# The gate projection of 2048 columns as one Strassen block with 1024-wide halves, in place of two plain jobs and one block with 512-wide halves

## The chip, the cores and the metric

The kernel runs on one core of one Trainium2 chip. The metric is device time in microseconds (us), the median of several executions. The engines are PE (matrix products), DVE (vector work), ACT (scalar work and casts), POOL and SP; in this kernel the last two mostly issue DMAs. Each engine takes its instructions strictly in the order in which they stand in its own program.

## The reference

One decoder layer for 512 rows of 2048 fp32 values. Only the last lines belong to the change:

```
x2  = x + merged @ w_out
g   = sigmoid(x2 @ w_ple_gate)          # 512 x 2048 times 2048 x 2048
x3  = x2 + g * (p @ w_ple)
out = x3 / sqrt(mean(x3^2) + 1e-6) * final_g
```

## The kernel before

**Arithmetic.** Every fp32 product is made of three products on PE: both operands are split into a rounded high part and a rest, and high·high, high·low and low·high are added in PSUM. A weight's high part is a cast on ACT (`hi`, `hs`, `th`, line 191), its low part a subtraction on DVE (`lo`, `ls`, `tl`, line 197). One matmul has 128 rows of x2 (a "row tile" t, four in all) by 512 columns.

**Jobs.** A projection is cut into jobs, which one generator, `gemm`, turns into a single stream of matmuls. A plain job ("N") has 512 columns and runs over 16 slices k of 128 rows of the weights: 16 x 4 x 3 = 192 matmuls. A Strassen job ("S") takes two halves of columns, two halves of the depth and two halves of the rows, and makes 7 products of sums of blocks in place of 8 products of blocks. Its work comes in units of 12 matmuls (one product, two slices k, two row tiles), and each unit needs one weight tile of 128x1024 (512 KB), which is a block of w_ple_gate or a sum of blocks. The gate projection is three jobs: `pg0` (plain, columns 0 to 511), `pg1` (Strassen, columns 512 to 1535 as two halves of 512, 28 units, 336 matmuls) and `pg3` (plain, the last 512): 720 matmuls.

**Order.** `fill(n)` lets the generator run n steps of three matmuls, and the lines between two calls stand in the program at that place. `split_to(i)` issues the cast and the subtraction for a unit two units ahead of its matmuls; there are three buffers for `hs`, three for `ls` and three for raw weights, so a cast waits until PE is through with the unit three before it. `background` is a queue of small pieces that `pop` takes out during the matmuls, `deferred` holds pieces for the next unit. The sums of x2 that Strassen's products need on the activation side are made by DVE in the background, and partly go through DRAM. SP issues the weight loads as raw buffers come free. During the mixers, `slow_one` issues one DMA at a time on POOL that forms sums of weights in DRAM for the output projection and others (line 411 paces it).

**End.** `pg3` is built with `tail=8`: the last 8 slices k are split in advance (`th`, `tl`), and the matmuls then go row tile by row tile, 24 for each t. After each of them `evac_last` runs: tanh on ACT, two operations on DVE that add the gated embedding onto x2 (`ple_add`, lines 1039 and 1042), the sum of squares (ACT, line 1082), a square root (line 1090), a reciprocal (DVE, line 1091), four multiplications by the root and `final_g` (line 1097), and the output's DMAs. Tanh and square root need different function tables on ACT, so there are table loads (lines 1080 and 1113, each issued by a `warm` operation on one column). Row tiles 0 to 2 are finished while PE works on the next. For the last row tile the products with `final_g` are made ahead (`final_weigh`, line 1066). After the last gate matmul PE only has `probe`, 41 small matmuls that nothing waits for.

## Time and profile before

| | |
|---|---|
| median of three executions | 1507.71 us (1507.51 to 1508.45) |
| span of the profiled execution | 1505.6 us |
| PE busy | 1499.0 us (100%) |
| DVE busy | 1244.3 us (83%) |
| ACT busy | 869.2 us (58%) |
| POOL busy | 390.4 us (26%) |

The span runs from the first to the last instruction of the profiled execution; the median is 2.1 us above it. Matmuls are pipelined, so a busy PE is not PE at its peak. A row of the trace gives the start, the duration, the engine, the source line, the operation, and output and input by the program's names; in brackets stands the idle time of the engine just before it and what ended it.

### The profile page before, as it was taken

The page shows a single profiled execution, that of the slowest core. Times are in us where ns is not written, and L with a number is a line of the kernel's source. Part 1 is how long each engine was busy: PE and PEld are TensorE (multiplying, and loading weights), DVE is VectorE, ACT ScalarE, POOL GpSimd, SP SyncE. Part 2 cuts the span into 40 slices and gives each one's busy share as a digit, 9 for nine tenths or more (in the row PEclk, how much of TensorE's full clock was granted, in tenths as well). Part 3 has the DMA queues.
Part 4 walks back from the last instruction along what each step waited for, and adds up shares of the span by engine and source line. Part 5 has one row for each costly group of instructions (what it writes and reads, how often), then busy time and mean ns, then how long its engine had stood idle before and what let it go on. Part 6 is the DMA issues. An engine that isn't in the chain of part 4 may idle for free.

```text
span 1505.6 us, 20508 instructions
## 1 busy us (share of the span) xinstructions
PE 1499.0 (100%) x7190; PEld 1253.5 (83%) x7190; DVE 1244.3 (83%) x1882; ACT 869.2 (58%) x1501; POOL 390.4 (26%) x608
## 2 busy tenths in 40 slices
PE   9999999999999999999999999999999999999998
PEld 8988888888888888888888888888888888888886
DVE  7987879999997888878888888887877985688877
ACT  6554567777765555555665555555546555444556
POOL 1321044343432332432343424330100011100000
PEclk9999999999999999999999999999999999999999
DMA  8889579789877795978595959896897779945555
GB/s 320 218 240 297 149 171 219 167 192 272 189 196 251 222 289 152 280 176 253 149 293 157 281 156 286 247 290 235 295 322 248 229 195 348 307 164 183 182 201 190
DMA packets 183703, 346.82 MB, mean 230 GB/s; under 512 B 15016, under 2 KB 75056, under 8 KB 180400
## 3 DMA queue, kind: packets, MB, share of 16 engines
q0 software_dynamic: 70544, 172.61, 41.9%
q1 hardware_dynamic: 112912, 172.64, 35.7%
q8 instruction: 56, 0.92, 0.2%
q14 instruction: 47, 0.39, 0.1%
q10 hardware_dynamic: 144, 0.26, 0.0%
HBM read 283.08 MB, written 109.58 MB: 261 GB/s over the span
## 4 chain that ended last, share of the span: by engine, by line
PE 98%; DVE 1%; ACT 1%; issue 0%; POOL 0%; POOLq 0%; ACTq 0%
PE ps_m L455 7%; PE ps_m L454 7%; PE ps_m L453 7%; PE ps_wo L454 3%; PE ps_wo L453 3%; PE ps_wo L455 3%; PE ps_t L1477 2%; PE ps_za L480 2%; PE ps_za L481 2%; PE ps_za L482 2%; PE ps_q L480 2%; PE ps_q L481 2%; PE ps_q L482 2%; PE ps_kv L453 2%; PE ps_kv L454 2%; PE ps_kv L455 2%
## 5 line engine op out<-in xcount | busy, mean ns | idle before, releaser
L197 DVE TENSOR_TENSOR ls<-b,hs 128x1024 fp32r<-128x1024 f32 x224 | 273.6, 1222 | 111.0 <-ACT hs L191 109.8
L191 ACT CAST hs<-b 128x1024 fp32r<-128x1024 f32 x224 | 235.5, 1053 | 204.2 <-PE ps_m L455 50.7
L191 ACT CAST hs<-raw 128x1024 fp32r<-128x1024 f32 x130 | 137.0, 1055 | 132.5 <-issue 33.7
L197 DVE TENSOR_TENSOR ls<-raw,hs 128x1024 fp32r<-128x1024 f32 x130 | 158.7, 1221 | 45.8 <-ACT hs L191 45.5
L453 PE MATMUL ps_m<-hs,act_h 128*128 128x512 f32 x256 | 100.1, 391 | 0.0
L455 PE MATMUL ps_m<-hs,act_l 128*128 128x512 f32 x256 | 99.7, 389 | 0.0
L454 PE MATMUL ps_m<-ls,act_h 128*128 128x512 f32 x256 | 99.6, 389 | 0.0
L333 DVE TENSOR_TENSOR b<-raw,b 128x1024 f32<-128x1024 f32 x76 | 92.5, 1218 | 1.6 <-DMA raw<-in_w_in_dram 1.6
L197 DVE TENSOR_TENSOR lo<-raw,hi 128x512 fp32r<-128x512 f32 (+1 forms) x120 | 79.7, 668 | 15.1 <-PE ps_pg L494 5.5
L191 ACT CAST hi<-raw 128x512 fp32r<-128x512 f32 (+1 forms) x120 | 70.6, 596 | 30.1 <-PE ps_pg L495 10.7
L333 DVE TENSOR_TENSOR b<-b,b 128x1024 f32<-128x1024 f32 x72 | 87.6, 1217 | 0.0
L191 ACT CAST pth<-ps_t 128x512 fp32r<-128x512 f32 (+1 forms) x88 | 47.6, 544 | 46.4 <-PE ps_t L1477 45.8
L1436 ACT ACTIVATE prob<-prob,st 128x512 f32<-128x512 f32 (+3 forms) x128 | 70.7, 556 | 5.2 <-DVE st L1427 5.1
L197 DVE TENSOR_TENSOR ptl<-ps_t,pth 128x512 fp32r<-128x512 f32 (+1 forms) x88 | 55.5, 635 | 7.9 <-ACT pth L191 7.2
L411 POOL COPY pad_r<-pad_r 128x1 f32<-128x1 f32 x39 | 31.0, 794 | 115.9 <-ACT pad_r L410 115.9
L1427 DVE CUSTOM_DVE_ANT_0 prob<-ps_s,b 128x512 f32<-128x512 f32 (+3 forms) x128 | 56.1, 484 | 4.4 <-PE ps_s L1418 4.1
L455 PEld LDWEIGHTS ps_m<-hs,act_l 128*128 128x128 f32 x256 | 48.0, 188 | 10.0
L454 PEld LDWEIGHTS ps_m<-ls,act_h 128*128 128x128 f32 x256 | 48.1, 188 | 9.9
L453 PEld LDWEIGHTS ps_m<-hs,act_h 128*128 128x128 f32 x256 | 48.1, 188 | 9.9
L480 PE MATMUL ps_za<-act_h,hi 128*128 128x512 f32 x128 | 54.0, 421 | 0.0
L1452 DVE TENSOR_SCALAR prob<-prob,st,gates 128x512 f32<-128x512 f32 (+3 forms) x128 | 51.8, 457 | 1.8
L480 PE MATMUL ps_q<-act_h,hi 128*128 128x512 f32 x128 | 52.1, 407 | 0.0
(752 smaller groups left out, 4554.4 us busy)
## 6 DMA issues: line engine op xcount, KB each, us to landing
raw<-in_w_in_dram SPq DMA_DIRECT2D x112, 512.0 KB, 5.5
b<-in_w_in_dram SPq DMA_DIRECT2D x58, 512.0 KB, 6.9
o<-in_w_out_dram POOLq DMA_DIRECT2D x48, 512.0 KB, 7.7
t<-in_w_up_b_dram POOLq DMA_DIRECT2D x24, 512.0 KB, 9.9
raw<-in_w_ple_gate_dram SPq DMA_DIRECT2D x24, 512.0 KB, 3.9
b<-o SPq DMA_DIRECT2D x18, 512.0 KB, 6.2
o<-o POOLq DMA_DIRECT2D x16, 512.0 KB, 6.3
act_l<-gate POOLq DMA_DIRECT2D x8, 1024.0 KB, 12.7
```

Source lines behind the costliest of these rows:

```text
L191: nc.scalar.copy(hi, src)
L197: nc.vector.tensor_tensor(out=lo, in0=src, in1=hi.bitcast(F32), op=ALU.subtract)
L333: nc.vector.tensor_tensor(out=b[o], in0=b[x], in1=b[y], op=ALU.subtract)
L453: nc.tensor.matmul(o, ah, wh, start=st, stop=False, skip_group_check=go)
L454: nc.tensor.matmul(o, ah, wl, start=False, stop=False, skip_group_check=go)
L455: nc.tensor.matmul(o, al, wh, start=False, stop=sp, skip_group_check=go)
L480: nc.tensor.matmul(ps, hi[:, j], ah, start=st, stop=False)
L481: nc.tensor.matmul(ps, hi[:, j], al, start=False, stop=False)
L482: nc.tensor.matmul(ps, lo[:, j], ah, start=False, stop=sp)
L1427: nc.vector.tensor_tensor_reduce(out=pt[:, j * n:j * n + n], in0=o[:, j], in1=b0[:, 512 - n:], scale=-SLOPE[h], scalar=3.0e38, op0=ALU.add ...
L1436: nc.scalar.activation(sl, sl, AF.Exp, bias=st[:, 0, j, hh:hh + 1], scale=-1.0, accum_out=st[:, 1, j, hh:hh + 1])
L1452: nc.vector.tensor_scalar(out=sl, in0=sl, scalar1=st[:, 1, j, hh:hh + 1], scalar2=gates[:, i, gate:gate + 1], op0=ALU.mult, op1=ALU.mult)
```

## The change

The three jobs become one Strassen job `pg` whose halves are 1024 columns wide. Each product now has 8 weight tiles u = 0 to 7 (four pairs of slices k, two blocks cb of 512 columns). The list `WIDE` gives the order of 52 units, and product 4's second column block comes at the end as four weight tiles split in advance, row tile by row tile, for rows 256 to 511 only. That is 52 x 12 + 2 x 24 = 672 matmuls.

Where the weight tiles come from: products 1, 2 and 3 use plain blocks. Product 7 reads `gate_sums`, which 16 more POOL DMAs (`slow_one`) form in DRAM during the mixers; each mixer group has two more places for them. b11+b12 for product 5 is added by DVE for u below 4 and by a DMA that adds into SBUF for the other four (tag "T"). Product 6 adds b22 by DVE (line 356), product 4 adds b21 by an adding DMA on POOL (line 441). The sums of x2 are now made from tiles `whole`, copied out of PSUM by ACT.

The output is finished in quadrants: a (rows 0 to 255, columns 0 to 1023), b (same rows, other columns), c (rows 256 to 511, columns 1024 on) and d (the rest). Quadrants a, b and c get their tanh, embedding and squares in the background, and rows 0 to 255 are multiplied and stored in the background too (`roots`, `put_row`). Rows 256 to 511 are finished at the end by `end_row`, once for each of two row tiles.

```diff
+WIDE = ([(p, u) for us in (range(4), range(4, 8)) for p in "21" for u in us] + [("5", u) for u in range(8)]
+        + [(p, u) for u in range(8) for p in "63"] + [("7", u) for u in range(8)] + [("4", u) for u in (0, 2, 4, 6)])
...
+            if job.wide is not None and k == "1" and n < 4:
+                load_to(ld["b12", n])
+                t = raw[ld["b12", n]]
+                nc.vector.tensor_tensor(out=t, in0=t, in1=raw[ld["b11", n]], op=ALU.add)
+            if job.wide is not None and k == "6":
+                nc.gpsimd.dma_start(raw[ld["b12", n]], wide_weights(job, "b21", n), accum_op=ALU.add)
...
+    def wide_units(job, si):
...
+        for n, (p, u) in enumerate(order):
+            flush()
+            split_to(si + state["ahead"] + max(0, n - len(order) + 4))
+            run_behind()
+            pop()
...
+        split_to(si + 3)
+        tails = [parts.pop(si + j) for j in range(4)]
+        for t in range(2):
+            o = sets[0][2 + t]
+            for k in range(8):
...
+                flush()
+                pop()
+                yield
+            job.tail(o, t)
...
+    def finish_last(t, cb, ps):
...
+        nc.scalar.activation(sg, ps, AF.Tanh, scale=0.5)
+
+        def add_on():
+            ple_add(x2, ple, sg)
+            nc.scalar.activation(sg, x2, AF.Square, accum_out=ss[:, 2 + t, 2 * cb:2 * cb + 1])
+        if cb:
+            add_on()
+        else:
+            deferred.append(add_on)
...
+    def put_row(t, half):
+        o = wide_rows("xab"[0] + "ab"[half])[:, t]
+        nc.vector.scalar_tensor_tensor(out=o, in0=o, scalar=rest[:, 0, t:t + 1], in1=columns_g(half), op0=ALU.mult, op1=ALU.mult)
+        nc.sync.dma_start(out[t * P:t * P + P, 1024 * half:1024 * half + 1024], o)
...
+    def end_row(ps, t):
...
+        finish_last(t, 1, ps)
         nc.scalar.activation(warm, eps_t, AF.Sqrt)
...
-    add_job(Job("pg0", "N", w_ple_gate, 0, 512, KT, h_act, evac_first, zs))
-    add_job(Job("pg1", "S", w_ple_gate, 512, 512, KT, gate_act, evac_quad(final_sg, place_sg), ("o", "s", "t")))
-    add_job(Job("pg3", "N", w_ple_gate, 1536, 512, KT, h_act, evac_last, ("s", "s", "g", "g"), tail=8))
+    pg = Job("pg", "S", w_ple_gate, 0, 512, KT, gate_act, evac_wide, (("o", "s"), ("t", "g")), order=WIDE, bank_of=WIDE_BANK, wide=gate_sums)
+    pg.tail = end_row
+    add_job(pg)
...
+    slow.extend(lambda u=u: nc.gpsimd.dma_start(gate_sums[:, u], wide_weights(jobs[-1], "b22", u)) for u in range(8))
+    slow.extend(lambda u=u: nc.gpsimd.dma_start(gate_sums[:, u], wide_weights(jobs[-1], "b12", u), accum_op=ALU.add) for u in range(8))
...
+        if n == 43:
+            assert not background
+            background.extend([nothing, partial(roots, 0)] + [partial(put_row, t, half) for t in range(2) for half in range(2)])
...
+    background.extend([nothing] * 8 + [partial(weigh_rows, "c", 1), partial(weigh_rows, "d", 1, slice(0, 512))])
+    finish("pg")
```

ACT before, the end of its program for the third row tile and the start of the last (`sg` is the tanh's output, `p_h_13627` the x2 tile of the last 512 columns):

```order
L1079 ACTIVATE sg<-ps_pg_13480 128x512
L1080 ACT_TABLE_LOAD
L1080 ACTIVATE warm<-eps_t 128x1
L1082 ACTIVATE sg,small<-p_h_13627 128x512
L1090 ACTIVATE rs<-small,rs 128x1
L1113 ACT_TABLE_LOAD
L1113 ACTIVATE warm<-eps_t 128x1
L1079 ACTIVATE sg<-ps_pg_13481 128x512
```

The table load and its `warm` stand between a row tile's tanh and its square here.

ACT after, the end of its program from the last cast of the tail on (`ps_pg_12715` and `ps_pg_12716` are product 4's first column block for the two row tiles, `ps_pg_12746` its second block for t=0):

```order
L196 CAST ob_h<-b_12938 128x1024
L1197 ACTIVATE sg<-ps_pg_12715 128x512
L1197 ACTIVATE sg<-ps_pg_12716 128x512
L1166 ACTIVATE p_h_13569,small<-p_l_13449 128x1024
L1201 ACTIVATE sg,small<-x 128x512 x2
L1166 ACTIVATE p_h_13569,small<-p_l_13449 128x1024
L1197 ACTIVATE sg<-ps_pg_12746 128x512
L1201 ACTIVATE sg,small<-x 128x512
L1236 ACT_TABLE_LOAD
L1236 ACTIVATE warm<-eps_t 128x1
L1241 ACTIVATE small<-small 128x1
```

Four squares (line 1166 twice, line 1201 twice) now stand between the last cast and the tanh of the row tile t=0, and the table load stands behind that row tile's square, where before it stood ahead of it.

DVE before, from the last weight splits to the first row tile's reciprocal:

```order
L197 TENSOR_TENSOR tl<-raw,th 128x512 x5
L1066 TENSOR_TENSOR p_l_13223<-p_l_13223,p_h_13542 128x512
L1066 TENSOR_TENSOR x_1_13474<-x_1_13474,p_h_13542 128x512
L1074 TENSOR_REDUCE rs<-small 128x4
L1075 TENSOR_SCALAR rs<-rs 128x4
L1039 SCALAR_TENSOR_TENSOR sg<-sg,s_13540 128x512
L1042 SCALAR_TENSOR_TENSOR p_h_13627<-sg,p_h_13627 128x512
L1066 TENSOR_TENSOR p_l_13301<-p_l_13301,p_h_13542 128x512
L1091 RECIPROCAL rs<-rs 128x1
```

The last five subtractions of weights stand together, and the products with `final_g` for the last row tile (line 1066) stand ahead of the first row tile's reciprocal.

DVE after, the same stretch (line 202 with `s_13452` or `p_h_13453` is a tail part's subtraction, line 1221 a `put_row`, lines 1154 and 1155 are `ple_add`):

```order
L202 TENSOR_TENSOR ls<-b_12929,hs 128x1024
L1221 SCALAR_TENSOR_TENSOR p_h_13004<-p_h_13004,small,p_h_13180 128x1024
L202 TENSOR_TENSOR ls<-b_12935,hs 128x1024
L202 TENSOR_TENSOR s_13452<-b_12581,ob_h 128x1024
L1154 SCALAR_TENSOR_TENSOR p_h_13569<-p_h_13569,s_13255 128x1024
L1155 SCALAR_TENSOR_TENSOR p_l_13449<-p_h_13569,p_l_13449 128x1024
L202 TENSOR_TENSOR s_13452<-b_12654,ob_h 128x1024
L202 TENSOR_TENSOR p_h_13453<-b_12932,ob_h 128x1024
L1154 SCALAR_TENSOR_TENSOR p_h_13569<-p_h_13569,s_13255 128x1024
L1155 SCALAR_TENSOR_TENSOR p_l_13449<-p_h_13569,p_l_13449 128x1024
L202 TENSOR_TENSOR p_h_13453<-b_12938,ob_h 128x1024
L1154 SCALAR_TENSOR_TENSOR sg<-sg,p_l_13570 128x512
```

The multiplications of rows 0 to 255 and quadrant c's embedding now stand between the last subtractions of weights, and the last of those is followed at once by quadrant d's embedding.

DVE after, from the reciprocal of row tile t=0 to the last one:

```order
L1242 RECIPROCAL small<-small 128x1
L1247 SCALAR_TENSOR_TENSOR x<-x,small,p_h_13180 128x512
L1247 SCALAR_TENSOR_TENSOR p_l_13449<-p_l_13449,small,p_h_13180 128x512 x2
L1247 SCALAR_TENSOR_TENSOR x<-x,small,p_h_13180 128x512
L1226 TENSOR_TENSOR p_l_13449<-p_l_13449,p_h_13180 128x1024
L1226 TENSOR_TENSOR x<-x,p_h_13180 128x512
L1154 SCALAR_TENSOR_TENSOR sg<-sg,p_l_13570 128x512
L1155 SCALAR_TENSOR_TENSOR x<-sg,x 128x512
L1226 TENSOR_TENSOR weighed<-x,p_h_13180 128x512
L1242 RECIPROCAL small<-small 128x1
```

The products with `final_g` for the last row tile (line 1226, the `weigh_rows` of the last lines of the diff) now stand behind the four multiplications of t=0 and ahead of the last row tile's embedding.

## Rows read from the trace of the kernel before

**Rows 1.** The page's first part: busy time, share, instructions of each engine.

```profile
PE 1499.0 (100%) x7190; PEld 1253.5 (83%) x7190; DVE 1244.3 (83%) x1882; ACT 869.2 (58%) x1501; POOL 390.4 (26%) x608
```

**Rows 2.** The page's chain of work that ended last, shares by engine.

```profile
PE 98%; DVE 1%; ACT 1%; issue 0%; POOL 0%; POOLq 0%; ACTq 0%
```

**Rows 3.** Windows, gate stage: length, busy PE, PEld, DVE, ACT, POOL; clock, DMA share, GB/s.

```profile
1330.00:1505.60 175.60, 171.30 (x780) 140.27 (x779) 140.08 (x187) 88.95 (x145) 11.68 (x17) 1.00 0.53 183
```

**Rows 4.** Timeline of PE, 50 matmul intervals in the job `pg3` apart.

```profile
1462.17 0.39 PE L493 MATMUL ps_pg<-hi,act_h 128*128 128x512 f32 x1
...
1473.51 0.39 PE L495 MATMUL ps_pg<-hi,ob_h 128*128 128x512 f32 x1
```

**Rows 5.** Timeline of PE's weight loads, the one wait in `pg3`.

```profile
1478.10 0.19 PEld L511 LDWEIGHTS ps_pg<-tl,act_h 128*128 128x128 f32 x1 [0.32 <-DVE tl L197]
```

**Rows 6.** Timeline of ACT, casts of `pg1` at a unit's pace.

```profile
1425.02 1.05 ACT L191 CAST hs<-raw 128x1024 fp32r<-128x1024 f32 x1 [1.67 <-PE ps_pg L455]
1427.74 1.05 ACT L191 CAST hs<-b 128x1024 fp32r<-128x1024 f32 x1 [1.67 <-PE ps_pg L455]
```

**Rows 7.** Timeline of DVE in `pg1`: large operations back to back, and a wait.

```profile
1369.43 1.22 DVE L333 TENSOR_TENSOR b<-b,b 128x1024 f32<-128x1024 f32 x1
1370.57 1.22 DVE L197 TENSOR_TENSOR ls<-b,hs 128x1024 fp32r<-128x1024 f32 x1
...
1419.52 1.28 DVE L860 TENSOR_TENSOR p_h<-ps_pg,keep 128x512 f32<-128x512 f32 x2
...
1426.10 1.23 DVE L197 TENSOR_TENSOR ls<-raw,hs 128x1024 fp32r<-128x1024 f32 x1 [0.36 <-ACT hs L191]
```

**Rows 8.** Timeline of DVE in `pg3`: 512-column operations back to back.

```profile
1466.83 0.68 DVE L1039 SCALAR_TENSOR_TENSOR p_h<-p_h,ple 128x512 f32<-128x512 f32 x1
1467.55 0.69 DVE L1042 SCALAR_TENSOR_TENSOR x<-p_h,x 128x512 f32<-128x512 f32 x1
1468.15 0.68 DVE L1039 SCALAR_TENSOR_TENSOR p_h<-p_h,ple 128x512 f32<-128x512 f32 x1
```

**Rows 9.** Timeline of PE, the last matmul of the gate projection.

```profile
1495.47 0.39 PE L512 MATMUL ps_pg<-th,act_l 128*128 128x512 f32 x1
```

**Rows 10.** Timeline of ACT at the end: the third row tile, then the last's tanh.

```profile
1490.45 0.60 ACT L1079 ACTIVATE sg<-ps_pg 128x512 f32<-128x512 f32 x1 [0.79 <-PE ps_pg L512]
1491.07 1.28 ACT L1080 ACT_TABLE_LOAD   x1
1492.36 0.20 ACT L1080 ACTIVATE warm<-eps_t 128x1 f32<-128x1 f32 x1
1492.53 0.64 ACT L1082 ACTIVATE sg<-p_h 128x512 f32<-128x512 f32 x1
1493.07 0.18 ACT L1082 ACTIVATION_READ_ACCUMULATOR sg<-p_h 128x1 f32 x1
1493.29 0.29 ACT L1090 ACTIVATE rs<-small,rs 128x1 f32<-128x1 f32 x1
```

**Rows 11.** Timeline of DVE at the end: multiplications, last embedding, last reciprocal.

```profile
1494.48 0.74 DVE L1097 SCALAR_TENSOR_TENSOR x<-x,rs,p_h 128x512 f32<-128x512 f32 x1
1495.15 0.75 DVE L1097 SCALAR_TENSOR_TENSOR p_l<-p_l,rs,p_h 128x512 f32<-128x512 f32 x1
...
1499.06 0.17 DVE L1091 RECIPROCAL rs<-rs 128x1 f32<-128x1 f32 x1 [0.39 <-ACT rs L1090]
```

**Rows 12.** DMA issues of weights and weight sums: count, size, median us to landing.

```profile
raw<-in_w_ple_gate_dram SPq DMA_DIRECT2D x24, 512.0 KB, 3.9
o<-o POOLq DMA_DIRECT2D x16, 512.0 KB, 6.3
...
b<-in_w_ple_gate_dram SPq DMA_DIRECT2D x8, 512.0 KB, 9.7
```

**Rows 13.** Windows in the mixers, where `slow_one` runs; columns as in rows 3.

```profile
800.00:900.00 100.00, 100.00 (x449) 82.81 (x448) 81.68 (x87) 57.88 (x86) 34.51 (x56) 1.00 0.78 216
980.00:990.00 10.00, 10.00 (x48) 8.31 (x46) 8.34 (x10) 6.70 (x9) 3.76 (x7) 1.00 1.04 365
```

More of the change, by code (lines that the diff above doesn't have):

```diff
@@ L282 @@
     raw, parts = {}, {}
-    state = {"loads": 0, "sum": 0, "high": 0, "low": 0, "ahead": 0, "more": 1, "pops": 2, "due": 0, "b11": 0, "late": 0, "rate": 0, "step": None, "slot": None}
+    state = {"loads": 0, "sum": 0, "high": 0, "low": 0, "ahead": 0, "more": 1, "pops": 2, "due": 0, "b11": 0, "late": 0, "rate": 0, "T": 0, "step": None, "slot": None}
     def ring(i, dtype, n=2):
@@ L310, in load_next @@
                 return
[L311 removed]
+            if loads[state["loads"]][0] != "raw" and {"b11": "free", "T": "T"}.get(loads[state["loads"]][0], "pool") not in quad:
                 if not quad.get("b12"):
@@ new lines, with finish_rows, squares @@
+    quads = {"a": (0, 0), "b": (0, 1), "c": (1, 1), "d": (1, 0)}
+    keeps = {}
+    def finish_rows(q, t):
+        top, half = quads[q]
+        sg, x2, ple = (wide_rows(n + q)[:, t] for n in ("sg", "x", "ple"))
+        def squares():
+            nc.scalar.activation(sg, x2, AF.Square, accum_out=ss[:, 2 * top + t, half:half + 1])
+        def add_on():
+            ple_add(x2, ple, sg)
+            later(squares)
+        nc.scalar.activation(sg, sg, AF.Tanh, scale=-0.5 if half else 0.5)
+        deferred.append(add_on)
@@ L2098, in stream_places @@
[L2098 to L2109 removed]
+                nc.scalar.copy(w[:, i], b)
@@ new lines, in turn_x2, with part_at, parts_at, third_sum @@
+            if each:
+                each(j, pair)
+            fill(units[j // 2])
+    def part_at(p, c):
+        v = home(p, c // 2)
+        return (v[:, i, 2 * (c % 2):2 * (c % 2) + 2] for i in range(2))
+    def parts_at(p, c, src):
+        parts_later(*part_at(p, c), src)
+    def third_sum(c):
+        a = whole[0, c]
+        o = stream.tile([P, 2, 256], F32, tag="lo", name="third", bufs=3)
+        sub(o, a[:, :, lo_t], a[:, :, hi_t])
+        if c > 1:
+            parts_at("7", c, o)
+            return
+        hi, lo = (stream.tile([P, 2, 256], F32R, tag=tag, name="third", bufs=n) for tag, n in (("hi", 4), ("lo", 3)))
+        def store():
+            for i, t in enumerate((hi, lo)):
+                nc.gpsimd.dma_start(s3x_dram[:, i, 2 * c:2 * c + 2], t)
+        parts_later(hi, lo, o, store)
```

447 lines of the change are left out of this document (249 added, 198 removed).

## The prediction

> **What bounds the kernel now.** I read four views. The page's first part shows PE busy for 1499.0 of 1505.6 us, DVE at 83%, ACT at 58% [rows 1]. The chain of work that ended last is PE for 98%, DVE and ACT for 1% each [rows 2]. In the windows the gate stage, from 1330 us to the end, has the same balance: PE 171.30 us busy, DVE 140.08, ACT 88.95, the granted clock 1.00 throughout, DMA engines busy to 0.53 [rows 3]. The timelines then show PE as a stream without gaps: 50 intervals between matmuls take 1473.51 - 1462.17 = 11.34 us, 0.2268 us each [rows 4]; the only wait that I found in the last 300 us is 0.32 us for a low part in `pg3` [rows 5]. So a matmul removed is 0.2268 us won, as long as weights and sums come in time, and what comes after the last matmul counts in full. Before, that end is short: the last gate matmul ends at 1495.47 + 0.39 = 1495.86 [rows 9], the last reciprocal starts at 1499.06 [rows 11], 3.2 us later. What follows it (three multiplications, the output's DMAs) is the same in both kernels.
>
> **Term 1, fewer matmuls.** 720 - 672 = 48, times 0.2268: **-10.9 us**. The wait of 0.32 us in `pg3` goes with it; the weight load runs ahead of its matmul, so some 0.2 us of it reached PE: **-0.2 us**.
>
> **Term 2, DVE at the end of the stream: +1.0 us.** A unit takes 12 x 0.2268 = 2.72 us on PE, and that is the pace at which the casts start: 1425.02, 1427.74 [rows 6]. The cast for unit n starts when PE leaves unit n-3, since there are three buffers; its subtraction on DVE starts 1.1 us later (1425.02 to 1426.10 [rows 6, 7]). Hence the subtraction for unit 47 can start 1.1 us into unit 45. From there DVE owes, in its own order, ahead of the last tail part's end:
> - 9 subtractions of 1024 columns (units 47 to 51, four tail parts), one every 1.14 us (1369.43 to 1370.57 [rows 7]): 10.3;
> - 4 `put_row` of 1024 columns. 512-column ones come every 0.67 us [rows 11], against 0.60 between independent operations with tensor operands (1467.55 to 1468.15 [rows 8]), so 1.14 + 0.07 = 1.21 each: 4.8;
> - 4 sums out of PSUM, 0.64 each (1.28 for two [rows 7]): 2.6;
> - quadrant c's embedding, two pairs. A dependent second operation costs 0.1 more (0.72 against 0.60 [rows 8]), so 1.14 + 1.24 a pair: 4.8.
>
> Together 22.4, plus the 1.1 of the cast, plus 0.7 that I allow for hand-overs (one such wait is 0.36 [rows 7]): the last tail part is ready 24.2 us after unit 45 began. PE wants it after 7 units (19.05) and three quarters of the first tail row tile (18 matmuls, 4.08), with its own start 23.2. PE then waits about **1.0 us**. Ends: 0.5 to 1.5 with prices 0.05 either way on some twenty operations; 0 if the hand-overs hide and the `put_row` run at 1.14.
>
> **Term 3, what follows the matmuls: +8.4 us.** Times are from E, the end of row tile t=0 of the tail.
> - The tanh of t=0 should start at E. But four squares stand ahead of it on ACT, and these wait for embeddings that DVE only reaches behind the last subtraction. That one ends 1.5 us before E (6 matmuls of 0.2268, a hand-over). Then DVE does two pairs of 512 columns at 0.60 + 0.72 = 1.32 each, to E + 1.2. Behind them ACT still has two squares, one of 512 columns (0.54 + 0.18 with its reading [rows 10]) and one of 1024 (about 1.05): tanh at E + 3.2.
> - Tanh 0.60, two operations of DVE 0.72 and 0.72 with hand-overs of 0.1: E + 5.5. Square and reading 0.8: E + 6.3.
> - Only now the table load, 1.28, and `warm`, 0.20 [rows 10]: E + 7.8. Before, both lay between tanh and square, hidden behind DVE's two operations. Square root 0.29 and reciprocal: E + 8.4.
> - Four multiplications at 0.67 [rows 11]: E + 11.1. Then the products with `final_g`, 1.14 and 0.61: E + 12.8, and only behind them the embedding of t=1: E + 14.2.
> - Square 0.8, table load and `warm` 1.48, root 0.4: the last reciprocal at E + 17.0.
>
> The last row tile's matmuls ended at E + 24 x 0.2268 = E + 5.4. So 11.6 us pass where 3.2 did: **+8.4 us**. If DVE had no arrears, the tanh of t=0 would start at E + 0.2, the rest would follow as listed, and the reciprocal would come at about E + 13.5: 13.5 - 5.4 - 3.2 = **+4.9**, the lower end. PE's wait in term 2 and this term share a cause, DVE's queue.
>
> A rule of the Trainium skill ("ScalarE: Activation LUTs", "What ACT_TABLE_LOAD costs") prices a switch of tables at about 1.28 us for the load and 1.38 us of draining beside it. The trace agrees with the load and shows no drain here: the load stands 0.02 us behind the end of the tanh (1490.45 + 0.60, load at 1491.07 [rows 10]). By the page term 3 would be larger by 2 x 1.38 = 2.8 us, an estimate from its figure.
>
> **Term 4, the start of the stage: +0.5 us.** In its first ten units DVE carries, for units 4 to 8, a subtraction and a sum of weights (2.28 us of a unit's 2.72) and the low parts of the last quarter of x2, some 13.6 us in 13.4 us of PE time; this can push a subtraction late by 0.2 us, or by nothing where the two units of lead absorb it. At the same time POOL loads about 3 MB for the row ends, and SP loads weights. A weight load lands in 3.9 us when alone and in 9.7 in a burst [rows 12]; two units of lead and a third raw buffer cover about 2 us of the 5.8 more: up to 3.8 late, once. The adding DMAs have 6.3 us in the nearest row [rows 12], and up to three units of time. From 0 to 3.8, I take 0.5, since the DMA engines are at 0.53 in this stage [rows 3].
>
> **Priced at nothing.** The 16 extra DMAs in the mixers. `slow_one` already issues such transfers, and with the DMA engines full (1.04 at 980 us, 0.78 over 800 to 900) PE still shows no gap [rows 13]. They move 16 x 0.5 MB, at 365 GB/s 1.4 us each at least, 23 us, and 16 x 6.3 = 101 at most, into a stage with a quarter of its DMA time free. The copies of x2 on ACT: ACT is busy 88.95 of 175.60 us [rows 3]. If that cover fails, a late copy costs up to 1.05 us once.
>
> **Sum.** 1505.6 - 10.9 - 0.2 + 1.0 + 8.4 + 0.5 = 1504.4 us of span. The median is 2.1 above the profiled span, so 1506.5 us: 1.2 less than 1507.71, 0.08%. A measurement of this kernel can tell about 0.2%, 3.0 us, from no change, so the bounds are 1504.7 and 1510.7.
>
> **Rivals.**
> - *Faster: the end costs only its plain order.* If DVE keeps up with its queue in the last units (the DVE windows say 80% busy on average, which speaks for it; the 24.2 against 23.2 us above speaks against), term 2 is 0 and term 3 is 4.9: 1507.7 - 10.9 - 0.2 + 4.9 = 1501.5. It decides from about 2 us less than my sum.
> - *Slower: weights come late in the first ten units.* POOL's row loads and SP's weight loads meet, each late weight tile costs PE 3.8 us. For it: 9.7 us in a burst [rows 12]. Against it: share 0.53. From two such tiles on it decides: 1506.5 - 0.5 + 7.6 = 1513.6.
> - *Slower: the mixers.* The extra transfers delay a load that PE waits for, by 6.3 us each [rows 12]; two of the sixteen give 1506.5 + 12.6 = 1519. The full DMA engines at 980 us are for it, PE's unbroken 10.00 of 10.00 there against it.
> - *The end with draining at each table load.* It would give the two exposed loads at the end an idle time beside them that no row has; from the rows it would have to lie in the 0.02 us ahead of 1491.07 [rows 10], so the rows give 1506.5 again, and at the very most, with a load's own 1.28 as idle twice, 1509.1. The Trainium skill's page above is where this rule stands.
>
> **How the numbers follow.** My sum: 0.56, with its own range 1504 to 1509, of which a fifth (0.11) lies below 1504.7. The faster rival: 0.20. Late weights: 0.13, of which 0.02 stay within the bounds. The mixers: 0.06. The drain: 0.05. Faster 0.20 + 0.11 = 0.31; slower 0.11 + 0.06 = 0.17; the same 0.52. For eight in ten the range takes half of the faster rival's side, down to 1502, and single late tiles, up to 1510.5.
>
> **What would show it.** 48 rows fewer on PE, at 0.2268. In the tail, idle time of about 1 us before a PE row that names the last low part. ACT's tanh of t=0 some 3 us behind the last matmul of its row tile, the table load behind the square, and the last reciprocal 11 to 12 us behind the last gate matmul; if it is 8 or less, term 3 is wrong and the faster rival right. In the first ten units no idle time of PE over 0.5 us; idle time that names a weight load or an adding DMA there, or any in the mixers, makes the slower rivals right.

## The result and the profile after

The change made the kernel slower: 1528.03 us (1527.41 to 1531.78, 4 runs) against 1507.62 us for the kernel before on the same chip (1507.51 to 1508.45, 4 runs), 20.4 us, ratio 1.014 with a 95% interval of 1.0125 to 1.0154. The profiled execution has a span of 1526.6 us, 21.0 more than before.

The page's first part and the shares of the chain that ended last, of the changed kernel (before: [rows 1, 2]):

```profile
PE 1496.8 (98%) x7142; PEld 1243.1 (81%) x7142; DVE 1238.8 (81%) x1841; ACT 880.2 (58%) x1502; POOL 423.2 (28%) x647
...
PE 86%; DVE 5%; DMA 4%; ACT 2%; issue 2%; POOL 0%; DVEq 0%; SPq 0%; ACTq 0%; POOLq 0%
```

The 48 matmuls are gone (7190 to 7142), but PE no longer sets the end alone. The view of waits names what PE waited for (total, times, longest, in us):

```profile
PE ps_pg L496 <- DVE ls L202: 7.4, 13, 0.8
PE ps_pg L495 <- ACT hs L196: 2.8, 2, 2.2
PE ps_pg L495 <- DVE p_h L1184: 1.5, 1, 1.5
...
PE ps_wo L551 <- ACT hs L196: 1.4, 1, 1.4
PE ps_pg L511 <- DVE p_h L202: 1.4, 1, 1.4
```

**Where the 21.0 us are.** I set four marks in both traces, the first matmul of the output projection (`ps_wo`), the first and the last of the gate projection, and the span's end. Up to the output projection: 1170.09 against 1168.88, +1.2. Output projection: 164.9 against 161.6 us, +3.3. Gate projection: 174.8 against 165.4, +9.4, where 10.9 less was due, so PE lost some 20 us there. From the last gate matmul's end to the span's end: 16.84 against 9.79, +7.05. Before, the gate projection went from 1330.51 to 1495.86 us [rows 9]; its first and its last matmul after (timeline of PE):

```profile
1334.98 0.39 PE L495 MATMUL ps_pg<-hs,ob_l 128*128 128x512 f32 x1
...
1509.37 0.39 PE L512 MATMUL ps_pg<-ob_h,p_l 128*128 128x512 f32 x1
```

Below, the loss of some units is the time from their first matmul to the first one behind them, less 0.2268 us for each interval. Units are counted from 0.

**The start of the gate projection.** Timeline of PE around the first long wait:

```profile
1352.87 0.39 PE L497 MATMUL ps_pg<-hs,act_h 128*128 128x512 f32 x1
1355.48 0.50 PE L495 MATMUL ps_pg<-hs,act_h 128*128 128x512 f32 x1 [2.22 <-ACT hs L196]
1356.74 0.65 PE L496 MATMUL ps_pg<-ls,act_h 128*128 128x512 f32 x1 [0.76 <-DVE ls L202]
1357.19 0.63 PE L497 MATMUL ps_pg<-hs,act_h 128*128 128x512 f32 x1
1357.62 0.63 PE L495 MATMUL ps_pg<-hs,act_h 128*128 128x512 f32 x1
```

The cast that PE waits for (1354.38, below) waited itself for a weight tile. Besides the wait the clock fell: after the idle time the matmuls come every 0.43 us in place of 0.227 (1.2 GHz in place of 2.4; the granted clock of 1355 to 1360 us is 0.69) until 1360.2, in which PE is busy again but slow. From 1352.87 to 1364.82 the next 25 intervals take 11.95 us where 5.67 would do: 6.3 us, and 1.0 in the wait after, 7.3 together. The same stretch on POOL and SP, and the two casts that came late (ACT):

```profile
1338.97 1.09 POOL L2305 DMA_DIRECT2D x<-x_d  x2
1345.38 1.05 POOL L2305 DMA_DIRECT2D s<-spill  x2 [5.32 <-PE ps_x L2211]
1348.12 1.07 POOL L2337 DMA_DIRECT2D ob_l<-s3x_d  x2 [1.69 <-PE ps_pg L497]
...
1346.65 0.37 SPq L329 DMA_DIRECT2D raw<-in_w_ple_gate_dram  x1
...
1354.38 1.04 ACT L196 CAST hs<-raw 128x1024 fp32r<-128x1024 f32 x1 [5.65 <-DMA raw<-in_w_ple_gate_dram]
1359.13 1.04 ACT L196 CAST hs<-raw 128x1024 fp32r<-128x1024 f32 x1 [3.70 <-DMA raw<-in_w_ple_gate_dram]
```

POOL issues 3 MB of row tiles and third sums there, and a weight tile issued at 1346.65 is in use only at 1359.13, 12.5 us later (3.9 was the median of before [rows 12]).

**Units 9 to 15.** Timelines of ACT and DVE for one unit of that stretch:

```profile
1367.19 1.05 ACT L196 CAST hs<-raw 128x1024 fp32r<-128x1024 f32 x1
...
1370.13 0.62 ACT L196 CAST p_h<-b 128x512 fp32r<-128x512 f32 x1 [1.89 <-DVE b L636]
1370.65 1.04 ACT L196 CAST hs<-raw 128x1024 fp32r<-128x1024 f32 x1
...
1368.27 1.22 DVE L202 TENSOR_TENSOR ls<-raw,hs 128x1024 fp32r<-128x1024 f32 x1 [1.04 <-ACT hs L196]
1369.41 0.68 DVE L636 TENSOR_TENSOR b<-b,b 128x512 f32<-128x512 f32 x1
```

This is a loop through two engines. The weight cast at 1367.19 releases the subtraction on DVE (1368.27), behind which stands the sum of x2 blocks (1369.41); that sum's cast (1370.13) stands on ACT ahead of the next weight cast (1370.65). One turn is 3.46 us, and a unit of PE 2.72. From 1363.73 to 1387.99 ACT makes seven turns in 24.26 us where 19.05 would do: 5.2 us. Neither engine is full, as the window of that stretch shows (columns as in [rows 3]):

```profile
1365.00:1392.00 27.00, 23.07 (x92) 16.63 (x93) 19.73 (x25) 14.83 (x20) 0.00 (x0) 1.00 0.39 125
```

**Units 20 to 23** wait for the adding DMAs (timeline of ACT, casts of their tiles):

```profile
1402.94 1.05 ACT L196 CAST hs<-b 128x1024 fp32r<-128x1024 f32 x1 [4.99 <-DMA b<-in_w_ple_gate_dram]
1406.94 1.05 ACT L196 CAST hs<-b 128x1024 fp32r<-128x1024 f32 x1 [1.90 <-DMA b<-in_w_ple_gate_dram]
1410.46 1.05 ACT L196 CAST hs<-b 128x1024 fp32r<-128x1024 f32 x1 [1.42 <-DMA b<-in_w_ple_gate_dram]
```

They come 4.0 and 3.5 us apart, not 2.72; from 1404.05 to 1418.18 PE's 48 intervals take 14.13 us where 10.89 would do: 3.2 us. **The last units and the tail** (timelines of ACT, DVE and PE):

```profile
1479.47 1.05 ACT L196 CAST hs<-raw 128x1024 fp32r<-128x1024 f32 x1 [3.34 <-DMA raw<-g]
...
1480.56 1.22 DVE L202 TENSOR_TENSOR ls<-raw,hs 128x1024 fp32r<-128x1024 f32 x1 [4.23 <-ACT hs L196]
...
1485.23 1.28 DVE L1184 TENSOR_TENSOR p_h<-ps_pg,keep 128x512 f32<-128x512 f32 x2
...
1481.84 0.50 PE L496 MATMUL ps_pg<-ls,p_l 128*128 128x512 f32 x1 [0.70 <-DVE ls L202]
1486.06 0.47 PE L495 MATMUL ps_pg<-hs,ob_l 128*128 128x512 f32 x1 [1.46 <-DVE p_h L1184]
1502.89 0.50 PE L511 MATMUL ps_pg<-p_h,p_l 128*128 128x512 f32 x1 [1.35 <-DVE p_h L202]
```

PE's third wait is that of term 2. The other two were not in the forecast. The second: product 4 adds on in the banks of product 7, whose sums DVE (line 1184) makes only behind a `put_row`, from 1485.23 on, 0.6 us after product 7's last matmul ended (1484.60). The first is a late weight tile once more: DVE stood idle for 4.23 us, for a cast that itself waited 3.34 us for a tile of `gate_sums`. **The end** (timelines of ACT and DVE; the last gate matmul ends at 1509.76):

```profile
1507.19 0.58 ACT L1197 ACTIVATE sg<-ps_pg 128x512 f32<-128x512 f32 x1
1509.26 0.63 ACT L1201 ACTIVATE sg<-x 128x512 f32<-128x512 f32 x1 [1.49 <-DVE x L1155]
1509.79 0.18 ACT L1201 ACTIVATION_READ_ACCUMULATOR sg<-x 128x1 f32 x1
1510.00 1.28 ACT L1236 ACT_TABLE_LOAD   x1
...
1514.57 1.22 DVE L1226 TENSOR_TENSOR p_l<-p_l,p_h 128x1024 f32<-128x1024 f32 x1
...
1520.20 0.16 DVE L1242 RECIPROCAL small<-small 128x1 f32<-128x1 f32 x1 [1.76 <-ACT small L1241]
```

Tanh 2.9 us behind the end of its row tile (1504.3), the table load behind the square, the products with `final_g` ahead of the last embedding, as forecast; the last reciprocal is 10.4 us behind the last gate matmul (11.6 forecast, 3.2 before). The load starts 0.03 us behind the end of the reading (1509.79 + 0.18). The rule of the Trainium skill ("ScalarE: Activation LUTs", "What ACT_TABLE_LOAD costs") would have put about 1.38 us of draining beside it; this trace does not show them either.

### The profile page after: what moved, and what is told of

It is laid out like the page before. It is cut to its first block, busy times and chain, and to the rows that moved or that the text cites. A ratio compares the mean times of both kernels' runs of the same rounds, so it can differ in the third digit from the quotient of the medians.

```text
span 1526.6 us, 20422 instructions
## 1 busy us (share of the span) xinstructions
PE 1496.8 (98%) x7142; PEld 1243.1 (81%) x7142; DVE 1238.8 (81%) x1841; ACT 880.2 (58%) x1502; POOL 423.2 (28%) x647
## 4 chain that ended last, share of the span: by engine, by line
PE 86%; DVE 5%; DMA 4%; ACT 2%; issue 2%; POOL 0%; DVEq 0%; SPq 0%; ACTq 0%; POOLq 0%
PE ps_m L551 7%; PE ps_m L553 7%; PE ps_m L552 7%; PE ps_wo L552 3%; PE ps_wo L551 3%; PE ps_wo L553 3%; PE ps_t L1615 2%; PE ps_za L578 2%; PE ps_za L579 2%; PE ps_za L580 2%; PE ps_kv L551 2%; PE ps_u L553 2%; PE ps_kv L553 2%; PE ps_ub L553 2%; PE ps_ub L552 2%
## 5 line engine op out<-in xcount | busy, mean ns | idle before, releaser
L202 DVE TENSOR_TENSOR ls<-raw,hs 128x1024 fp32r<-128x1024 f32 x154 | 188.2, 1222 | 75.7 <-ACT hs L196 75.4
L196 ACT CAST hs<-raw 128x1024 fp32r<-128x1024 f32 x154 | 162.1, 1054 | 144.1 <-issue 35.2
L370 DVE TENSOR_TENSOR b<-raw,b 128x1024 f32<-128x1024 f32 x68 | 82.9, 1219 | 1.4 <-DMA raw<-in_w_in_dram 1.3
L370 DVE TENSOR_TENSOR b<-b,b 128x1024 f32<-128x1024 f32 x64 | 78.0, 1218 | 0.0
L460 POOL COPY pad_r<-pad_r 128x1 f32<-128x1 f32 x55 | 43.0, 789 | 111.4 <-ACT pad_r L459 111.4
L202 DVE TENSOR_TENSOR lo<-raw,hi 128x512 fp32r<-128x512 f32 (+1 forms) x96 | 63.2, 664 | 6.3 <-ACT hi L196 5.2
L196 ACT CAST hi<-raw 128x512 fp32r<-128x512 f32 (+1 forms) x96 | 56.1, 591 | 17.4 <-PE ps_vcg L593 4.9
```

What stands on the lines that cost most here:

```text
L196: nc.scalar.copy(hi, src)
L202: nc.vector.tensor_tensor(out=lo, in0=src, in1=hi.bitcast(F32), op=ALU.subtract)
L370: nc.vector.tensor_tensor(out=b[o], in0=b[x], in1=b[y], op=ALU.subtract)
L460: nc.gpsimd.tensor_copy(steps[:, 16 + i:17 + i], steps[:, i:i + 1])
```

## The experiments

My theories were: the DMA engines are overfull at the start (theory D), the loop through ACT and DVE (L), the order at the end (O), DVE's arrears in the last units (A), and the weight sums in the mixers (M). The rivals stand in each expectation. Times are medians against the kernel before in the same session (1507.3 to 1507.9). The runs of one changed version lie 2 to 6 us apart, so where a median moves by less, the argument goes by the rows of the profile, which is one execution.

**1. Transfers placed later.** `load_rows` for quadrant a stands at unit 10, the third sum's load at unit 24, both at unit 5 before:

```diff
         if n == 5:
             for f in (third_sum, sum_5, sum_6, sum_3):
                 tasks(f, 2, 3)
+        if n == 10:
             load_rows("a", "x", new_x())
             load_rows("a", "ple", new_s4(1, F32))
+        if n == 24:
             homes["7", 0] = ob_l[:, 0:4]
```

> POOL's transfers for quadrant a (2 MB) go from unit 5 to unit 10, product 7's third sum (1 MB) from unit 5 to unit 24; nothing else changes. Theory (these 3 MB take the DMA engines from the weights of units 4 to 8): the waits of 2.2 and 0.8 us at 1355 to 1357 us and the stretch at the lower clock behind them go, the median falls by 5 to 9 us from 1528.0. Rival (the weights alone, 1 MB for each of units 4 to 7, are too much for the DMA engines): the waits stay at half or more, the fall is under 3 us.

1526.77 us (1525.66 to 1530.41), the waits at the start 1.8 and 0.8 us. By its wording the rival won, but the kernel did not do what I meant (timeline of POOL in this run):

```profile
1343.88 1.09 POOL L2305 DMA_DIRECT2D x<-x_d  x2
1350.28 1.05 POOL L2305 DMA_DIRECT2D s<-spill  x2 [5.31 <-PE ps_x L2211]
```

The gate projection began at 1339.9 here, so POOL issued quadrant a's rows in the same units as before. POOL had only the buffers to wait for; a place in the program does not hold back an idle queue. Only the third sum (1 MB) had moved. That alone took the loss of units 4 to 7 from 6.3 to 3.6 us and the gate projection from 174.8 to 172.0; the median does not show it, since the output projection of this execution began at 1175.0 us in place of 1170.1. Experiment 6 does it properly.

**2. The casts behind the weight casts.** `behind` is an existing list that is run after `split_to`:

```diff
     def parts_at(p, c, src):
-        parts_later(*part_at(p, c), src)
+        parts_later(*part_at(p, c), src, at=behind if c > 1 and p in "7563" else deferred)
...
-        if n == 5:
+        if n == 4:
             for f in (third_sum, sum_5, sum_6, sum_3):
                 tasks(f, 2, 3)
+        if n == 5:
             load_rows("a", "x", new_x())
```

> The casts of the activation sums (products 7, 5, 6, 3 for the second half of the depth) stand on ACT behind the next unit's weight cast in place of ahead of it, and begin one unit earlier. Theory (a loop over two engines, weight cast, weight subtraction, sum, sum's cast, next weight cast, sets 3.46 us a unit): the eight waits of 0.45 us between 1366 and 1391 go, units there come every 2.72 us as far as the weights are there, the median falls by 4 to 6 us. Rival (these units only run without lead because the weights were late): units there stay at 3.4 us or the same time is lost to loads, the fall is under 1.5 us.

1521.46 us (1519.95 to 1522.53), 6.6 less than the changed kernel. Windows of the stretch of the loop, in this run:

```profile
1365.00:1392.00 27.00, 27.00 (x119) 22.33 (x118) 24.65 (x30) 17.34 (x22) 3.64 (x3) 0.99 0.70 211
```

PE is busy for all 27 us with 119 matmul rows (23.07 us with 92 in the changed kernel; columns as there). L holds. The waits at units 20 to 23 shrank to one of 0.3 us in this profile (a loss of 0.7 us), but that is not the edit by itself: with the same casts, the profiles of experiments 3, 5, 7 and 9 lose 3.0 to 4.2 us there. Why this one did not stays open.

**3. Both edits.**

> Both edits of the two kernels before. If the two losses are apart, their falls add up, to some 12 us, and the adding DMAs of units 20 to 23, which wait for the tiles that the sums free, come earlier, which takes up to 2.8 us more: 1513 to 1517. If both have one cause, the fall is that of the larger one alone: about 1520.

1519.61 us (1517.43 to 1521.74), within the scatter that of experiment 2 alone. Only the third sum had moved. In the profile units 4 to 7 lose 2.6 us in place of 7.3, and units 20 to 23 lose 3.9 in place of 0.7.

**4. The end in the other order.**

```diff
         nc.scalar.activation(sg, ps, AF.Tanh, scale=0.5)
+        if cb:
+            nc.scalar.activation(warm, eps_t, AF.Sqrt)
...
         if last:
             weighed = stream.tile([P, 512], F32, tag="lo", name="weighed", bufs=3)
             weigh_rows("d", t, second, weighed)
+        else:
+            weigh_rows("c", 1)
+            weigh_rows("d", 1, slice(0, 512))
+        for f in waiting:
+            f()
```

(The first row tile's `put` for columns 512 and 1536 goes into `waiting`; the `warm` of `end_row` and the line that put the products with `final_g` into `background` go.)

> At the end alone: the load of the square root's table stands between tanh and square, the products with final_g for the last row tile stand ahead of the first reciprocal (where DVE waits 2.5 us), and two of the first row tile's four multiplications stand behind the last embedding. Theory (the end's loss is an order of operations, and no amount of work): last reciprocal about 5 us behind the last gate matmul in place of 10.4, the median falls by 4 to 5.5 us. Rival (the end is late since DVE is behind with its queue): the fall is under 2 us.

Timeline of DVE in this run:

```profile
1517.43 0.15 DVE L1251 RECIPROCAL small<-small 128x1 f32<-128x1 f32 x1
```

This last reciprocal came 6.0 us behind the last gate matmul (which ended at 1511.41) in place of 10.4, and the end from there took 13.0 us in place of 16.8: O holds, for 3.8 of the 7.1 us. The median, 1525.82 us (1522.96 to 1526.79), fell by 2.2 only. This profile's output projection began 1.1 us later than that of the changed kernel, a scatter that theory M is about.

**5. The output projection's casts too.** On the kernel of experiment 2, `at=behind if p in "7563"`, whatever c.

> On the kernel with the casts moved (1521.5): in the output projection too, the casts of the sums for products 5, 6 and 3 stand behind the next weight cast on ACT. Theory (the two waits at 1311 to 1330 us, 1.4 and 0.4 us, are the same loop): they go, the time from the output projection's first matmul to the gate projection's first falls from 164.9 to 163 us. Rival (a single crowded unit on ACT or DVE): the waits stay.

1520.19 us (1518.46 to 1524.59). The waits at 1311 and 1330 us are gone, and from the first matmul of the output projection to the first of the gate projection it takes 161.6 us, as in the kernel before. So these 3.3 us were the order of the casts on ACT as well, though in two single waits and not in a loop that repeats. Units 20 to 23 lose 4.0 us here, so the median is within the scatter that of experiment 2.

**6. The transfers paced.** On that kernel, POOL is made to wait:

```diff
+    def pace(i):
+        nc.scalar.copy(steps[:, i:i + 1], eps_t)
+        nc.gpsimd.tensor_copy(steps[:, 16 + i:17 + i], steps[:, i:i + 1])
...
+        if n == 9:
+            pace(0)
             load_rows("a", "x", new_x())
             load_rows("a", "ple", new_s4(1, F32))
+        if n == 24:
+            pace(2)
...
-        if n == 17:
+        if n == 22:
+            pace(1)
             load_rows("b", "x", place("h0", F32))
```

> On the kernel with both groups of casts moved (1520.2): POOL's transfers for quadrant a wait for an ACT copy of unit 9, those for quadrant b for one of unit 22, product 7's third sum for one of unit 24. Before, POOL issued them as soon as their buffers came free, a at 1339 to 1348 us (units 1 to 5) and b right behind the adding DMAs of units 20 to 23; in the run that only placed them later in the program, POOL still issued quadrant a's at 1344 to 1350 us. Theory (these transfers collide with the weights): the waits at 1353 to 1360 us, the stretch at the lower clock and the four waits at 1396 to 1408 us go or shrink to under 2 us in all; the gate projection's first to last matmul falls from 168.2 to 159 to 162 us, the median to 1511 to 1514. Rival (the weight loads alone are too much, in units 3 to 8 and for the adding DMAs): it stays over 165 us, the median over 1517.

1519.59 us (1518.58 to 1520.63), the gate projection 167.9 us: no gain, so that by its numbers the rival won, and still the most telling run. Windows of it, where the first waits had been, where the transfers now stand, and at the adding DMAs:

```profile
1345.00:1360.00 15.00, 15.00 (x68) 12.43 (x67) 14.04 (x18) 8.53 (x13) 0.00 (x0) 1.00 0.82 273
1360.00:1380.00 20.00, 17.75 (x75) 13.59 (x74) 14.36 (x19) 11.40 (x17) 3.04 (x5) 1.00 0.67 232
1390.00:1410.00 20.00, 17.19 (x70) 12.49 (x69) 10.95 (x10) 10.47 (x17) 5.69 (x7) 1.00 0.78 186
```

Without POOL's rows the first units have no wait at all (units 4 to 7 lose nothing, 5.4 us in experiment 5): D is right about the cause, and the weights alone are not too much. But the waits come again at 1372 to 1378 us, behind the rows' new place at 1362.5, and the waits for the adding DMAs stay, though quadrant b's rows now come after them.

**7. Interleaved products,** on the kernel of experiment 2: `WIDE` begins with (2, u0 to u3), then (1,0), (2,4), (1,1), (2,5) and so on.

> On the kernel with the casts moved (1521.5): product 1's first four units take turns with product 2's last four, so that the units that need 1 MB of weights each no longer follow each other. Theory (the first waits are the rate of the weight loads themselves, 1 MB for each of four units of 2.72 us, 385 GB/s): the waits of 1.3 to 1.9 us between 1353 and 1363 us and the stretch at the lower clock shrink to under 1 us together; the gate projection, 165.6 us there, falls by 4 to 6 us, the median to 1516 to 1518. Rival (any order is late there, since POOL's 3 MB come in the same time): the waits stay within 1.5 us of what they were in sum.

1521.37 us (1520.10 to 1523.07): no change. There is one wait of 2.3 us at 1358 in place of two earlier; units 4 to 7 lose 5.2 us, where the same units in the old order lose 7.3, 5.4 and 5.5 us (experiments 2, 5 and 9), so the theory is out. That POOL's 3 MB are the cause, as the rival has it, experiment 6 shows more directly.

**8. Sums on DVE in place of adding DMAs,** on the kernel of experiment 5: product 5's tiles 4 to 7 load b12 and, through the raw buffers, b11 again, and `sum_to` adds them.

> On the kernel with both groups of casts moved (1520.2): the four sums b11 + b12 for units 20 to 23 are made by DVE from a second plain load of b11, in place of a POOL DMA that adds into SBUF. Theory (the four waits at 1396 to 1408 us, 2.9 us in sum, come from these adding DMAs, which take the DMA engines longer than plain loads: 1.1 of their time at 240 to 280 GB/s): they go, the gate projection falls from 168.2 to 165 to 166 us, the median by 2 to 3 us. Rival (they come from quadrant b's transfers or from the raw buffers): in the paced run, where quadrant b's transfers came after these units, the waits were 3.6 us, which speaks against the first; with the second they stay at 2 us or more, or grow, since two more raw loads stand in SP's queue.

1517.37 us (1517.04 to 1521.94), 2.8 less. One wait of 0.6 us is left at these units, which lose 0.9 us in place of 4.0. In the other profiles they lose 3.0 to 4.5 us with adding DMAs, but for experiment 2's 0.7, and 1.1 to 1.9 with sums on DVE (experiments 12 and 13). So the adding DMAs were most of the cause there. From 1380 to 1395 us the DMA engines moved 332 GB/s at a share of 0.92 in this run, and 261 at 0.95 in that of experiment 5.

**9. Rows 0 to 255 multiplied by the root on ACT,** on the kernel of experiment 2: `put_row` becomes `nc.scalar.mul`, and DVE multiplies by `final_g` ahead of it (quadrant a at units 28 and 29).

> On the kernel with the casts moved (1521.5): rows 0 to 255 are multiplied by final_g on DVE (quadrant a at units 28 and 29, b at units 45 and 46) and by the root on ACT, in place of four operations on DVE in units 45 to 48. DVE has 2.6 us less to do there. Theory (DVE's queue is what PE waits for at 1477.7, 1.3 us, and at 1494.5, 1.35 us): the second wait goes, the first gets shorter, the median falls by 1.5 to 3 us. Rival (ACT's casts become late in turn, or the waits come from late weights): under 0.8 us.

1523.33 us (1520.71 to 1526.01), no gain by the median. In the profile the tail's wait fell from 1.35 to 0.36 us, so A holds for that one; the wait for product 7's sums stayed at 1.3 us, since the product with `final_g` now stands ahead of them where the `put_row` stood, and waits at the start and in the mixers scattered by more than the microsecond won.

**10. The weight sums in the mixers.** First the changed kernel without them: the 16 DMAs and their two places in each mixer group are left out, and product 7 uses the plain block b22.

> On the changed kernel (1528.0): the 16 added DMAs that sum weights in DRAM during the mixers, and the two more places for them in each mixer group, are left out; product 7 is computed with the plain block b22 in place of the sum, loaded in the same size. Theory (these DMAs make the mixers' own loads late): no PE wait in the mixers over those of the kernel before, the output projection's first matmul at 1168.9 us as there (1170.1 to 1175.0 in the runs with the DMAs), the median falls by 1.2 to 5 us, and the scatter of several us between runs goes. Rival (the mixers lose nothing, the scatter is the gate stage's): that matmul stays at 1170 or later.

1528.01 us (1527.22 to 1529.98), no gain. Its profile, which is of the longest of its four runs, has two waits in the mixers (0.7 and 0.3 us, at 868 and 871 us), and the output projection begins at 1170.6 us. By the signs of the expectation M did not show. Then the other way round, the kernel before with the DMAs added and their result unused:

```diff
+    slow.extend(lambda u=u: nc.gpsimd.dma_start(gate_sums[:, u], gate_block("b22", u)) for u in range(8))
+    slow.extend(lambda u=u: nc.gpsimd.dma_start(gate_sums[:, u], gate_block("b12", u), accum_op=ALU.add) for u in range(8))
...
-        return [first, nothing, nothing, slow_one, normal, nothing if g < 4 else slow_one, affine, second,
-                nothing, nothing, spatial, slow_one, nothing, turn]
+        return [first, slow_one, nothing, slow_one, normal, nothing if g < 4 else slow_one, affine, second,
+                slow_one, nothing, spatial, slow_one, nothing, turn]
```

> The kernel before (1507.5) with one part of the change alone: the 16 DMAs that sum gate weights in DRAM and the two more places for them in each mixer group; the sums are not used. Theory (they make the mixers' own POOL loads late by up to some us, differently in each run): 1509 to 1512, with a scatter of over 1 us between runs, and waits of PE on the mixers' tiles. Rival (they are hidden, and the later start of the output projection has another cause): 1507.3 to 1508, no wait in the mixers.

1510.82 us (1508.70 to 1512.63, 11 runs) against 1507.25 (1506.56 to 1508.07, 15 runs), ratio 1.0023 (1.0014 to 1.0032). Timeline of DVE in it:

```profile
877.44 0.69 DVE L1915 TENSOR_TENSOR mix_u<-mix_u,mix_z 128x512 f32<-128x512 f32 x1 [2.47 <-DMA mix_z<-zb_d]
```

A load that a mixer's gate needs comes late, and PE waits 1.8 us behind it. M holds for this part alone, 3.6 us, with a scatter of 4 us where the kernel before has 1.5. The changed kernel has the same late load (timeline of DVE), and behind it, at 981.04 us, the only wait of PE over 0.15 us between 400 us and the output projection, 0.57 us for `ps_ob`:

```profile
980.25 0.69 DVE L2046 TENSOR_TENSOR mix_u<-mix_u,mix_z 128x512 f32<-128x512 f32 x1 [2.21 <-DMA mix_z<-zb_d]
```

All twelve profiles with these DMAs in the mixers have a wait for `ps_ob` of 0.5 to 2.1 us at 980 to 985 us, and the four without them (the kernel before, the first run of this experiment, experiments 12 and 13) have none. So for this wait M holds in the changed kernel too. The two waits of this experiment's first run are others; why leaving the DMAs out did not lower the median stays open.

**11. All edits that had helped or were expected to.**

> The changed kernel with all edits that helped or are expected to: casts behind the weight casts, POOL's transfers paced, rows 0 to 255 multiplied by the root on ACT, the end in the other order. If the losses are apart, the sum is 1528.0 - 6.5 (casts of the gate) - 3.3 (casts of the output projection) - 7 (pacing) - 5 (end) - 1 (ACT) = about 1505, within 2 us of the kernel before on either side. If pacing fails, about 1512.

1518.42 us (1514.18 to 1519.79), above both figures of the expectation. The end and the tail behave as in experiments 4 and 9, but there is a new wait of 4.9 us at 1430.8, and units 24 to 46 lose 7.2 us. The timeline of DVE shows where it comes from:

```profile
1427.24 1.22 DVE L1228 TENSOR_TENSOR x<-x,p_h 128x1024 f32<-128x1024 f32 x1 [5.95 <-DMA p_h<-in_final_g_dram]
```

Experiment 9's edit wants `final_g` at unit 28. Its load, issued at 1410.55 behind the paced 3 MB of quadrant b's rows and the third sum, is in use 16.7 us later, and the subtractions of weights stand behind it on DVE. In experiment 9, where quadrant b's rows came earlier and the third sum long before, those units lost 0.2 us.

**12. Everything spread out.** Experiments 4, 5 and 8, POOL's transfers 1 MB at a time by `pace` at units 8, 11, 25, 28, 32 and 35, and the 16 DMAs issued by `slow_one` during the output projection.

> All that helped, and the transfers spread: casts behind the weight casts, the four sums on DVE, the end in the other order, POOL's transfers 1 MB at a time at units 8, 11, 25, 28, 32 and 35, and the 16 DMAs that sum gate weights issued during the output projection in place of the mixers. Theory (the change's losses are its DMA traffic in crowded places and orders of instructions, each mendable): 1520.2 - 2.9 (sums) - 4 (first units) - 4.4 (end) - 3.6 (mixers) = about 1505, below the kernel before. Rival (the traffic is too much wherever it stands, 1 MB more for each product with sums): the waits move to the output projection or to units 24 to 40, and the median stays over 1510.

1510.46 us (1508.14 to 1511.52, 11 runs), ratio 1.0019 (1.0010 to 1.0029). The output projection now begins at 1169.0 us, the gate projection takes 162.0 us. But in the output projection PE waits for the load of x2 (timeline of PE):

```profile
1278.78 0.96 PE L2222 MATMUL ps_x<-ident,x 128*128 128x128 f32 x7 [3.21 <-DMA x<-x_d]
```

By the wording of the expectation that is the rival.

**13. Spread around that load too,** with experiment 9's edit.

> The spread kernel (1510.5) with the 16 DMAs that sum gate weights thinned out around the load of x2 that PE waited for at 1278.8 us (3.2 us), about half of them ahead of it and half behind 1300 us, and with rows 0 to 255 multiplied by the root on ACT. Theory (that wait is these DMAs on POOL's queue and in the DMA engines): it goes, and 1 us of the last two DVE waits: 1505.5 to 1507, just below the kernel before. Rival (the traffic only moves its loss): a new wait of 2 us or more at 1300 to 1360 us, the median stays over 1509.

1511.09 us (1508.64 to 1513.08, 6 runs). That wait is gone. The view of waits shows others in its place:

```profile
PE ps_pg L495 <- DVE ls L202: 2.8, 3, 1.3
PE ps_pg L494 <- DVE p_l L202: 1.9, 1, 1.9
```

The rival holds: the rest moves. 17.6 of the 20.4 us (experiment 12) can be had back by order, place and sums on DVE, but no version here beat the kernel before.

## Why the prediction was wrong

**Term 1 was right.** 48 rows fewer on PE, and where nothing waits the matmuls still come every 0.227 us.

**Term 2 was right in mechanism and small.** The tail's wait is 1.4 us, 1.5 by PE's rows (1.0 forecast, ends 0 to 1.5). Units 47 and 48 cost 2.5 us more, which the step missed. 1.6 of it is the wait for product 7's sums, 0.6 us of that by DVE's queue and the rest the sum itself: the step asked only when the last tail part would be ready, not who else waits for DVE in between, namely product 4 for product 7's banks. The other 0.9 is no arrears of DVE, which stood idle for 4.23 us ahead of that subtraction, but a late weight tile. The queue was priced well: from unit 47's subtraction to the end of the last tail part it took 22.3 us (1480.56 to 1502.84), without a gap, against 22.4. But it began 4.2 us later than forecast (1.1 us into unit 45 is 1476.4), and PE lost 2.5 us meanwhile, so that the wait came out so near is partly luck.

**Term 3 was right,** 7.1 us against 8.4, with the forecast steps in the forecast order. Experiment 4 shows that 3.8 of it is order. The lower end of 4.9 has a slip: with the tanh at E + 0.2 in place of E + 3.2 the listed steps end at E + 14.0, not 13.5, so it is 5.4, and the faster rival 1502.0. Nothing hangs on it.

**Term 4 is the step that failed:** "From 0 to 3.8, I take 0.5, since the DMA engines are at 0.53 in this stage [rows 3]". The loss that it priced is 7.3 us late weights, 5.2 us loop and 3.2 us adding DMAs, 15.7 us; with the 1.5 us of the tail and the 2.5 us of units 47 and 48 these are 19.7 of the some 20 us that the gate projection lost. Three errors are behind that sentence.
- The share 0.53 is that of the kernel before. The change itself adds traffic, and I gave it no share. Windows of 145 us of the gate projection, of the changed kernel and (second fence) of the one before:

```profile
1335.00:1480.00 145.00, 135.35 (x578) 107.09 (x577) 97.67 (x104) 71.51 (x92) 24.47 (x30) 0.99 0.83 247
```

```profile
1330.00:1475.00 145.00, 145.00 (x649) 120.27 (x649) 119.09 (x150) 68.64 (x108) 9.54 (x13) 1.00 0.55 185
```

- POOL's 3 MB were taken as spread over the first ten units. POOL had only free buffers to wait for and issued them within 10 us (1339 to 1348), on the four units that need two weight tiles each. The 12.5 us for one tile lie over the 9.7 that was taken as the bound; that row gives the median of eight loads, which is no bound.
- DVE's work for units 4 to 8 was summed (13.6 us in 13.4), and from the sum I read a lag of 0.2 us; five units of 2.72 us are 13.6, so by its own prices there was none. The chain from ACT to DVE and back to ACT was never followed, and it set 3.46 us a unit with both engines partly idle. ACT's new work had been priced at nothing by a share, 88.95 of 175.60 us, with one late copy of 1.05 us as the worst case. The loop cost 5.2 us here, and the order of the casts 3.3 us in the output projection, whose new order on ACT I had not looked at.

**The mixers, priced at nothing:** 1.2 us in the profile, 3.6 us by the second run of experiment 10, though the first run, without the DMAs, won nothing. PE without gaps at a share of 1.04 [rows 13] did show that there was no wait then, but not how near the next load was to being late; the changed kernel's wait is in that very window, at 981 us.

**The rivals.** Late weights was the right place and side (1513.6 forecast, from two late tiles on). Its two tiles at 3.8 us are 7.6 us, and 7.3 us were measured, which is partly luck, since 1.6 of it is the lower clock, which it had left out. It fell short of 1528 since the loop, the adding DMAs and the output projection were in no rival. The mixers rival was right in kind, with 0.6 us of PE's wait in the profile where it had 6.3 for one late load. The faster rival, and the draining, showed nowhere.

## What to carry to other kernels

Price a change's own DMAs against the share of the stretch that they land in after the change, and find out what holds each issuing queue back: a queue that waits for nothing but free buffers issues as soon as they are free, even if the call stands later. Follow the order across engines in a circle (what does the next cast stand behind, and what does that wait for), since a loop can set a pace that no engine's busy time shows. A block scheme that saves 7% of a stage's matmuls but needs sums of weights and of activations pays in traffic and in waits, and at a PE without gaps each of these waits is a loss.
